# One block product in the first layer instead of two, turns from SBUF to SBUF, weight buffers of half a unit, and weight sums begun by an account of the transfers

## The chip, the cores and the metric

The kernel runs on one core of a Trainium2 chip. The metric is the device time of one execution in microseconds (us), the median of several runs. The engines named below are PE (TensorE, the matrix multiplications), DVE (VectorE), ACT (ScalarE), POOL (GpSimd) and SP (SyncE, which here only issues transfers). DMA engines carry the transfers; the queues of SP, ACT and POOL feed them.

## The reference

Two layers over 256 tokens of 2048 channels, float32. In each layer one wide projection (`w_in`, 2048 x 12304) makes the inputs of two groups of heads, a matrix memory (mLSTM) and a gated linear recurrence (RG-LRU); a second projection (`w_out`, 4096 x 2048) brings both back to 2048 channels.

```python
def hybrid_layer(x, ...):
    u = rms_norm(x, norm_g)
    p = u @ w_in
    qk, v, o, z_a, ig, fg, xb, z_b = jnp.split(p, SPLIT_AT, axis=-1)
    qk = silu(causal_dwconv(qk, qk_conv)); q, k = split(qk, 2)
    h = mlstm_chunkwise(q, k, v, ig + i_bias, log_sigmoid(fg + f_bias))
    h = h * sigmoid(o)                       # per head, then a norm over the head
    y_a = normed(h) * head_norm_g * silu(z_a)
    xc = causal_dwconv(xb, lru_conv_w) + lru_conv_b
    y_b = rg_lru(xc, w_a, b_a, w_x, b_x, lam) * silu(z_b)
    return x + concatenate([y_a, y_b]) @ w_out
# reference: two such layers, then a final rms_norm
```

## The kernel before

All products are float32 work done in three multiplications of rounded parts: each operand is split into a rounded part H (type fp32r) and the rest L, and `H*H + H*L + L*H` is summed in PSUM. The activations are split once per layer (`x_s`); the weights are split as they arrive: ACT casts `wH <- raw`, DVE subtracts `wL <- raw - wH`.

The weights come as 1 MB units, in the order in which they are used (`_sequence`). A unit is two halves of 512 KB. One plain half feeds 12 multiplications 128x512 (two token tiles, two slices of the contraction, three products), which PE works off in one go. Per layer there are four groups `g` of columns, each with the inputs `qk`, `v`, `o`, `z`, `xb`, `zb` of that group (four units each), the small gate products (`gate`, line 874), and the output projection of the group before (`out`). Loads are issued on SP into three buffers `raw` of one unit (`load_unit`, lines 339 and 341); splits run three halves ahead of PE (`AHEAD`), into four buffers `wH`, `wL`.

Block products: two columns of inputs of one layer (a pair in `PAIRS`) are multiplied together by seven block products instead of eight (a Strassen-Winograd scheme over two token tiles, two halves of the contraction and the pair). A pair has 7 x 4 = 28 block halves of 512 KB (`rawb`, loaded at line 349), each feeding 6 multiplications (lines 1229 to 1231, into the bank `ps_b`), where the plain form has 16 halves with 12 each. The block halves are placed among plain ones. The scheme needs sums of activation blocks (`block_sums`, on DVE, tiles `sums`, `sum_t`), an addition of each product into `res` (DVE), and sums of weight blocks in DRAM (`w_d`): `weight_sums` copies a block from the input into `w_d` (SP queue, line 1133) and adds further blocks by accumulating transfers (POOL queue, line 1142). It keeps a pace by PE's planned time (`PACE`: 6.5 us between transfers for the first layer, 10 for the second). Before, both pairs are done so in both layers: pair 0 is `v` and `o` of group 2, pair 1 is `o` and `z` of group 3.

A turn brings tokens on partitions to channels on partitions. ACT writes `tok`, DVE transposes blocks of 32x32 into `blk`, four transfers of 128 KB on SP (line 528) write a DRAM buffer `moved` with the blocks rearranged, and one transfer of 512 KB on POOL (line 529; the last turn on SP) reads it into `fr`. `fr` is then read by ACT (`ch`, `tok`, `zsg`) or DVE (`zb`). There are 35 turns. Their readers are placed by planned PE time (`LANDING` 10 us, `FAR` 15 us after the turn) and then by a scheduler that gives each engine its order.

Each engine and each queue works in order: what waits at the head holds back what is behind it. Transfers of one queue are counted on eight semaphores in rotation, and a transfer waits for the one eight before it on its queue.

Of the kernel before, what the change touches and what calls it, by code (L numbers as in the profile page):

```python
# [16 lines left out]
P = 128  # L17
# [15 lines left out]
PACE = 6.5, 10.0  # L33
# [64 lines left out]
def tile_trunk(ctx, tc, x, xt, par, gw, gb, ws, final_g, out):  # L98
# [22 lines left out]
    wraw = ctx.enter_context(tc.tile_pool(name="wraw", bufs=3))  # L121
# [7 lines left out]
    st = {"nload": 0, "lag": 0.0, "t": 0.0, "nprep": 0, "pair": 0, "aux": 0}  # L129
# [28 lines left out]
    def load_x_acc():  # L158
        new_x_acc()
        for c in range(4):  # L160
            nc.sync.dma_start(out=xa(c), in_=xd[c])

    def store_x(c):
        S.dma_start(out=xd[c], in_=xa(c))

# [157 lines left out]
    def load_unit(hf):  # L323
        n = st["nload"]
        st["nload"] += 1
        item, j = hf["at"]
        raw = hf["box"]["raw"] = wraw.tile([P, 2048], F32, tag="raw", name="raw")
        if n < 4:
            w = 512 if n == 0 else 1024
            u = blocks[item, j]  # L330
            for o in range(0, 2048, w):
                if o % 1024 == 0:
                    load_xt(n, o // 1024)
                nc.sync.dma_start(out=raw[:, o : o + w], in_=ws[u][:, o : o + w])
        elif hf["paired"]:
            o = 1024 * (j % 2)
            for s_ in range(2):
                u = blocks[item, 2 * s_ + j // 2]
                st["ld"] = nc.sync.dma_start(out=raw[:, 1024 * s_ : 1024 * s_ + 1024], in_=ws[u][:, o : o + 1024])
        else:  # L340
            st["ld"] = nc.sync.dma_start(out=raw, in_=ws[blocks[item, j]])
        if 3 <= n < 7:
            load_x(n - 3)

    def load_block(hf):
        if hf["made"]:
            require(hf["made"])
        raw = hf["raw"] = wblk.tile([P, 2, 512], F32, tag="rawb", name="rawb")
        st["ld"] = nc.sync.dma_start(out=raw.rearrange("p k n -> p (k n)"), in_=hf["from"])
        if "loaded" in hf:  # L350
            st[hf["loaded"]] = True

    def add_unit(mms, before=None, after=None, paired=False, own=None):
        box = {}
        halves.append([dict(box=box, i=i, mm=mms[i], split=None, paired=paired, own=own and own[i],
                            before=before if i == 0 else None, after=after if i == 1 else None) for i in range(2)])

    def prepare(hf):
        n = st["nprep"]
        if "from" not in hf:  # L360
# [5 lines left out]
            raw = hf["box"]["raw"]  # L366
        if "from" in hf:
            r = hf["raw"]
        elif hf["paired"]:
            r = raw.rearrange("p (s n) -> p s n", s=2)[:, :, 512 * hf["i"] : 512 * hf["i"] + 512]  # L370
        else:
            r = raw.rearrange("p (i n) -> p i n", i=4)[:, 2 * hf["i"] : 2 * hf["i"] + 2, :]
# [6 lines left out]
        for j, o in enumerate((slice(0, 1), slice(1, 2)) if opening else (slice(0, 2),)):  # L379
# [5 lines left out]
            if hf["own"] and "ends" in st:  # L385
                order(st["wH"], st["ends"][0])
                order(st["wL"], st["ends"][1])
        hf["split"] = (H.rearrange("p s n -> p (s n)"), L.rearrange("p s n -> p (s n)"))
# [129 lines left out]
    def swapped(tok, blk=None, back=G):  # L518
# [5 lines left out]
        st["lag"] += 1.2  # L524
        V.transpose(out=blk.rearrange("p m n -> p (m n)"), in_=tok.rearrange("p m c t j -> p (m c t j)"))
        moved = dram.tile([P, 4, 256], F32, tag="moved", name="moved", bufs=2)
        for a in range(4):
            nc.sync.dma_start(out=moved[:, a].rearrange("(m j) n -> j m n", m=4), in_=blk[32 * a : 32 * a + 32])
        i0 = back.dma_start(out=fr.rearrange("p a c t i -> p a (c t i)"), in_=moved)  # L529
# [479 lines left out]
    def out_chunk(l, g, c):  # L1009
# [9 lines left out]
        def postfn():  # L1019
            ps = acc()  # L1020
            if g < NG - 1:
# [3 lines left out]
                st["staged"] = st["n"]  # L1025
                return
# [38 lines left out]
    def block_sums(l):  # L1065
# [50 lines left out]
        yield from made(1, "S3", False, x(0, 0), x(1, 0), 4, (0, 3))  # L1116
        yield from made(1, "S1b", True, s(0), x(0, 0), 4, (1, 7))
        yield from made(0, "S4b", True, s(0), x(0, 1), 4, (1, 6))

    def block_unit(l, p, r, c, j):  # L1120
# [3 lines left out]
           for p in range(2)] for l in range(DEPTH)]  # L1124

    def weight_sums():

        def jobs(l, p):

            def copied(to, src, at, engine=nc.sync):  # L1130
                def f():
                    j, cs = at
                    i0 = engine.dma_start(out=wd[l][p][to][j][:, cs], in_=src(j)[:, cs])
                    order(i0, st["gq"] if engine is G else st["ld"])
                    if engine is G:
                        paced(i0, st["wH"])
                return f

            def added(to, src, at):
                def f():  # L1140
                    j, cs = at
                    i0 = G.dma_start(out=wd[l][p][to][j][:, cs], in_=src(j)[:, cs], accum_op=ALU.add)  # L1142
                    order(i0, st["gq"])
                    paced(i0, st["wH"])
                return f

            def b(r, c):
                return lambda j: block_unit(l, p, r, c, j)

            parts = [(j, slice(1024 * h, 1024 * h + 1024)) for j in range(2) for h in range(2)]  # L1150
            first, other, late = [], [], []
            for n, at in enumerate(parts):
                first += [(None, False, copied(0, b(0, 0), at), None), (None, True, added(0, b(0, 1), at), (5, n))]
                if p == 1:
                    first += [(None, True, copied(2, lambda j: wd[l][p][0][j], at, G), (5, n)),
                              (None, True, added(0, b(1, 1), at), (6, n))]
                else:
                    late.append((("loaded", l, p, 5, n), True, added(0, b(1, 1), at), (6, n)))
                other += [(None, False, copied(1, b(1, 1), at), None), (None, True, added(1, b(0, 1), at), (7, n))]
            late += [(("loaded", l, p, 6, n), True, added(0, b(1, 0), at), (4, n)) for n, at in enumerate(parts)]  # L1160
            return deque(first + other + late)

        queues = [jobs(l, p) for l in range(DEPTH) for p in range(2)]
        while st["n"] < SUMS_FROM:
            yield "wait"
        while any(queues):
            ready = [i for i, q in enumerate(queues) if q and (q[0][0] is None or q[0][0] in st)]
# [3 lines left out]
            i = ready[0]  # L1171
            _, adding, begin, made = queues[i].popleft()
            while adding and st["n"] - st.get("staged", -9) < 2 and not st.get("forced"):
                yield "wait"
            begin()
            if made:
                st[("made", i // 2, i % 2) + made] = True
            t0 = st["t"]
            while before(t0 + PACE[i // 2]):
                yield "wait"  # L1180
# [276 lines left out]
    for item, j in seq:  # L1457
        l, what = item[1], item[2:]
        if _blockwise(item):
            p = next(p for p in range(2) if what in PAIRS[p])  # L1460
# [5 lines left out]
    for l in reversed(range(DEPTH)):  # L1466
        for p in (1, 0):
# [19 lines left out]
    for n, hf in enumerate(order_):  # L1487
        st["n"] = n
        while nprep < len(order_) and nprep <= n + AHEAD:
            while st["nload"] < len(plain_) // 2 and st["nload"] <= (nplain + 5) // 2:  # L1490
                load_unit(plain_[2 * st["nload"]])
# [27 lines left out]
        st["t"] += took  # L1519
    drain()  # L1520
# [94 lines left out]
```

## Time and profile before

| | |
|---|---|
| median of 3 runs (1493.07 to 1495.65) | 1494.67 us |
| the profiled execution / its span | 1500.83 us / 1499.1 us |
| busy: PE / DVE / ACT / POOL | 98% / 80% / 65% / 9% of the span |
| granted TensorE clock, mean | 0.991 |
| moved by transfers | 425.39 MB, 284 GB/s over the span |

A busy PE here counts a multiplication from its start to its modelled end (390 ns), while the next one starts 0.227 us after it; so the share of 98% says little, and the number of multiplications in a stretch says more. Waits are put down to what ended last.

### The profile page before, as it was taken

How to read it: one execution, taken by the hardware profiler on the slowest of the kernel's cores; microseconds unless marked ns; L12 is line 12 of the kernel's file. 1: busy time of each engine (PE TensorE's matmuls, PEld its weight loads, DVE VectorE, ACT ScalarE, POOL GpSimd, SP SyncE). 2: the span in 40 equal slices, each digit the busy share in tenths (PEclk: the TensorE clock that was granted, in tenths of full speed). 3: DMA queues.
4: the chain of work that ended last, by engine and by line, in shares of the span. 5: the costliest groups of instructions: out<-in, count | busy, mean ns of one | idle time of the engine just before them, and what ended most of it. 6: DMA issues, size and time to landing. Idle time of an engine off the chain costs nothing. (4 is left out here: it accounts for less than half of the span.)

```text
span 1499.1 us, 19073 instructions
## 1 busy us (share of the span) xinstructions
PE 1470.4 (98%) x6734; PEld 1223.4 (82%) x6734; DVE 1194.8 (80%) x1678; ACT 981.2 (65%) x1256; POOL 142.0 (9%) x226
## 2 busy tenths in 40 slices
PE   9999999999989999999999999999999999999997
PEld 7888888888867888888887788888888888878876
DVE  5888898978677599877866888988787977888775
ACT  6666866567575667658564667665577757666665
POOL 0020101111101010000000200001000000000002
PEclk9999999999999999999999999999999999999999
DMA  9879999999999999899897787999978898777883
GB/s 353 325 257 277 302 306 301 323 318 287 333 282 281 295 312 313 289 304 305 295 331 230 228 289 250 309 283 296 290 264 299 259 268 265 271 262 239 248 303 109
DMA packets 117871, 425.39 MB, mean 284 GB/s; under 512 B 12928, under 2 KB 33424, under 8 KB 100368
## 3 DMA queue, kind: packets, MB, share of 16 engines
q1 hardware_dynamic: 95600, 348.39, 65.5%
q0 software_dynamic: 19712, 71.33, 21.9%
q10 hardware_dynamic: 2464, 4.47, 0.8%
q8 instruction: 52, 0.85, 0.2%
q14 instruction: 43, 0.35, 0.1%
HBM read 386.89 MB, written 91.77 MB: 319 GB/s over the span
## 5 line engine op out<-in xcount | busy, mean ns | idle before, releaser
L407 PE MATMUL acc<-wH,x_s 128*128 128x512 f32 x2496 | 786.1, 390 | 6.0 <-ACT wH L112 3.1
L112 DVE TENSOR_TENSOR wL<-raw,wH 128x1024 fp32r<-128x1024 f32 (+1 forms) x468 | 557.6, 1198 | 176.2 <-ACT wH L112 174.0
L112 ACT CAST wH<-raw 128x1024 fp32r<-128x1024 f32 (+1 forms) x468 | 481.0, 1035 | 289.0 <-PE acc L407 201.9
L407 PEld LDWEIGHTS acc<-wH,x_s 128*128 128x128 f32 x2496 | 469.7, 188 | 104.8 <-ACT wH L112 4.2
L407 PE MATMUL acc<-wL,x_s 128*128 128x512 f32 x1248 | 486.3, 391 | 3.5 <-DVE wL L112 3.5
L407 PEld LDWEIGHTS acc<-wL,x_s 128*128 128x128 f32 x1248 | 234.9, 188 | 53.4 <-DVE wL L112 5.3
L112 DVE TENSOR_TENSOR wL<-rawb,wH 128x1024 fp32r<-128x1024 f32 x112 | 136.4, 1218 | 38.7 <-ACT wH L112 38.6
L112 ACT CAST wH<-rawb 128x1024 fp32r<-128x1024 f32 x112 | 117.6, 1050 | 71.3 <-PE acc L407 47.2
L407 PE MATMUL acc<-wH,yaH 128*128 128x512 f32 x224 | 87.8, 392 | 0.0
L407 PE MATMUL acc<-wL,yaH 128*128 128x512 f32 x224 | 87.7, 391 | 0.0
L407 PE MATMUL acc<-wH,yaL 128*128 128x512 f32 x224 | 87.6, 391 | 0.0
L407 PE MATMUL acc<-wH,ybL 128*128 128x512 f32 x224 | 87.5, 390 | 0.0
L407 PE MATMUL acc<-wH,ybH 128*128 128x512 f32 x224 | 87.4, 390 | 0.0
L407 PE MATMUL acc<-wL,ybH 128*128 128x512 f32 x224 | 87.2, 389 | 0.0
L112 ACT ACT_TABLE_LOAD x63 | 80.8, 1283 | 9.4 <-DVE qc L112 3.5
L1142 POOL DMA_DIRECT2D w_d<-in_ws_dram x64 | 55.0, 859 | 298.9 <-ACT wH L112 183.4
L529 POOL DMA_DIRECT2D fr<-moved x34 | 19.3, 569 | 402.2 <-DMA moved<-blk 359.5
L112 DVE SCALAR_TENSOR_TENSOR qc<-ch,pars,qc 128x255 f32<-128x255 f32 (+2 forms) x96 | 42.3, 475 | 11.8 <-ACT qc L112 11.5
L1230 PE MATMUL ps_b<-wL,sums 128*128 128x512 f32 x128 | 50.0, 390 | 0.1
L1229 PE MATMUL ps_b<-wH,sums 128*128 128x512 f32 x128 | 50.1, 391 | 0.0
L1231 PE MATMUL ps_b<-wH,sums 128*128 128x512 f32 x128 | 49.9, 389 | 0.0
L407 PEld LDWEIGHTS acc<-wH,yaH 128*128 128x128 f32 x224 | 42.5, 190 | 8.9
(230 smaller groups left out, 1843.4 us busy)
## 6 DMA issues: line engine op xcount, KB each, us to landing
raw<-in_ws_dram SPq DMA_DIRECT2D x136, 1024.0 KB, 7.5
raw<-in_ws_dram SPq DMA_DIRECT2D x190, 512.0 KB, 6.8
w_d<-in_ws_dram POOLq DMA_DIRECT2D x64, 512.0 KB, 9.8
rawb<-w_d SPq DMA_DIRECT2D x64, 512.0 KB, 7.7
rawb<-in_ws_dram SPq DMA_DIRECT2D x48, 512.0 KB, 7.1
fr<-moved POOLq DMA_DIRECT2D x34, 512.0 KB, 7.4
moved<-blk SPq DMA_DIRECT2D x132, 128.0 KB, 4.4
w_d<-in_ws_dram SPq DMA_DIRECT2D x32, 512.0 KB, 8.6
```

The costliest lines, as they stand in the source:

```text
L112: ins = f(*a, **k)
L407: st["mm"] = PE.matmul(o, a_[:, kt, P * t : P * t + P], W[:, k], start=b, stop=z)
L529: i0 = back.dma_start(out=fr.rearrange("p a c t i -> p a (c t i)"), in_=moved)
L1142: i0 = G.dma_start(out=wd[l][p][to][j][:, cs], in_=src(j)[:, cs], accum_op=ALU.add)
L1229: PE.matmul(box["b"], aH, Hv[:, k], start=opening and k == 0, stop=False, skip_group_check=True)
L1230: PE.matmul(box["b"], aH, Lv[:, k], start=False, stop=False, skip_group_check=True)
L1231: PE.matmul(box["b"], aL, Hv[:, k], start=False, stop=kp == 3 and k == 1, skip_group_check=True)
```

## The change

Four things are changed. (1) `PRODUCTS = 1, 2`: the first layer has a block product for pair 0 alone; `o` and `z` of its group 3 go the plain way. (2) A turn no longer goes through DRAM: 16 transfers of 32 KB (32 partitions, 1 KB each) go from `blk` to `fr`, eight on SP and eight on POOL (all 16 on SP for the last one). (3) `raw` is six buffers of a half unit, each loaded by itself (`load_half`; the paired kinds `qk`, `xb`, `zb` by two transfers of 256 KB, the others by one of 512 KB). (4) `weight_sums` issues its copies too on POOL, in another order, and begins one when an account of transfer time, which each transfer raises and PE's planned time lowers, has room (`RATE`, `COPY`, `ADDING`, `TURN`), in place of `PACE`. The loads of `x_acc` are spread over eight halves.

```diff
-PACE = 6.5, 10.0
+RATE = 0.9, 0.75
+COPY, ADDING, TURN = 1.3, 2.6, 1.7
+PRODUCTS = 1, 2
...
-    return item[0] == "in" and any(item[2:] in pair for pair in PAIRS)
+    return item[0] == "in" and any(item[2:] in pair for pair in PAIRS[: PRODUCTS[item[1]]])
...
-    wraw = ctx.enter_context(tc.tile_pool(name="wraw", bufs=3))
+    wraw = ctx.enter_context(tc.tile_pool(name="wraw", bufs=6))
...
         for c in range(4):
-            nc.sync.dma_start(out=xa(c), in_=xd[c])
+            timed.append((st["n"] + 2 * c, lambda c=c: load_x_c(c)))
...
-    def load_unit(hf):
+    def load_half(hf):
         n = st["nload"]
         st["nload"] += 1
-        raw = hf["box"]["raw"] = wraw.tile([P, 2048], F32, tag="raw", name="raw")
+        (item, j), i = hf["at"], hf["i"]
+        raw = hf["raw"] = wraw.tile([P, 1024], F32, tag="raw", name="raw")
...
         elif hf["paired"]:
-            o = 1024 * (j % 2)
+            o = 1024 * (j % 2) + 512 * i
             for s_ in range(2):
                 u = blocks[item, 2 * s_ + j // 2]
-                st["ld"] = nc.sync.dma_start(out=raw[:, 1024 * s_ : 1024 * s_ + 1024], in_=ws[u][:, o : o + 1024])
+                st["ld"] = nc.sync.dma_start(out=raw[:, 512 * s_ : 512 * s_ + 512], in_=ws[u][:, o : o + 512])
         else:
-            st["ld"] = nc.sync.dma_start(out=raw, in_=ws[blocks[item, j]])
+            st["ld"] = nc.sync.dma_start(out=raw, in_=ws[blocks[item, j]][:, 1024 * i : 1024 * i + 1024])
+        st["dma"] += COPY
...
         V.transpose(out=blk.rearrange("p m n -> p (m n)"), in_=tok.rearrange("p m c t j -> p (m c t j)"))
-        moved = dram.tile([P, 4, 256], F32, tag="moved", name="moved", bufs=2)
-        for a in range(4):
-            nc.sync.dma_start(out=moved[:, a].rearrange("(m j) n -> j m n", m=4), in_=blk[32 * a : 32 * a + 32])
-        i0 = back.dma_start(out=fr.rearrange("p a c t i -> p a (c t i)"), in_=moved)
+        for m in range(4):
+            for a in range(4):
+                engine = nc.sync if m < 2 else back
+                i0 = engine.dma_start(out=fr[32 * m : 32 * m + 32, a].rearrange("p c t i -> p (c t i)"),
+                                      in_=blk[32 * a : 32 * a + 32, m])
...
+            def moved(to, src, at, **how):
+                def f():
+                    j, cs = at
+                    i0 = G.dma_start(out=wd[l][p][to][j][:, cs], in_=(wd[l][p][src][j] if src == 0 else block_unit(l, p, *src, j))[:, cs], **how)
+                    order(i0, st["gq"])
+                    paced(i0, st["wH"])
+                    st["dma"] += ADDING if how else COPY
+                return f
...
+            l, p, q = ready[0]
+            st["rate"] = RATE[l] if q[0][0] is None else 1.0
+            while (st["dma"] > (COPY if q[0][0] is None else ADDING) or st["n"] - st.get("staged", -9) < 2) and not st.get("forced"):
                 yield "wait"
...
-            while st["nload"] < len(plain_) // 2 and st["nload"] <= (nplain + 5) // 2:
-                load_unit(plain_[2 * st["nload"]])
+            while st["nload"] < len(plain_) and st["nload"] <= nplain + 5:
+                load_half(plain_[st["nload"]])
...
         st["t"] += took
+        st["dma"] = max(0.0, st["dma"] - took * st["rate"])
```

Three places show what it moves. The first is ACT at the turn of `qk` of group 2 in the first layer: `tok_...` begins the turn, `ch_...<-fr_...` reads it, the casts `wH` between them feed PE. Before:

```order
L112 ACTIVATE tok_3522<-acc_3326,rstd_465 128x4x4x32 x2
L112 CAST wH_3536<-rawb_3405 128x1024
L112 CAST wH_3548<-raw_3392 128x1024
L112 CAST wH_3568<-raw_3392 128x1024
L112 CAST wH_3584<-rawb_3482 128x1024
L112 ACT_TABLE_LOAD
L112 ACTIVATE E_3594<-E_3594 128x768
L112 CAST wH_3604<-raw_3447 128x1024
L112 CAST wH_3633<-raw_3447 128x1024
L112 CAST wH_3653<-raw_3503 128x1024
L112 CAST wH_3669<-rawb_3546 128x1024
L112 COPY ch_3621<-fr_3526 128x1024
```

And now, the same turn:

```order
L114 ACTIVATE tok_3743<-acc_3540,rstd_477 128x4x4x32 x2
L114 CAST wH_3770<-rawb_3621 128x1024
L114 CAST wH_3782<-raw_3607 128x1024
L114 CAST wH_3801<-raw_3639 128x1024
L114 CAST wH_3819<-rawb_3703 128x1024
L114 ACT_TABLE_LOAD
L114 ACTIVATE E_3829<-E_3829 128x768
L114 CAST wH_3839<-raw_3665 128x1024
L114 COPY ch_3855<-fr_3747 128x1024
```

The reader of the turn stood behind eight casts (five of plain halves, three of block halves) and now stands behind five (three and two).

The second place is POOL around the same turn (`E` is a mask for the attention scores, `nb` a broadcast load). Before:

```order
L529 DMA fr_3314<-moved_3316 128x1024
L1142 DMA w_d0101_126<-in_ws_dram 128x1024 x2
L1133 DMA w_d0121_130<-w_d0101_126 128x1024
L665 AFFINE_SELECT E_3594<-E_3594 128x128 x4
L529 DMA fr_3526<-moved_3528 128x1024
L1142 DMA w_d0101_126<-in_ws_dram 128x1024
L1142 DMA w_d0110_127<-in_ws_dram 128x1024
L529 DMA fr_3765<-moved_3767 128x1024
```

And now:

```order
L532 DMA fr_3515<-blk_3514 32x256 x8
L654 DMA nb_3765<-nG_d0_119 128x512
L696 MEMSET vH_3972 128x4x2
L1140 DMA w_d1001_126<-in_ws_dram 128x1024
L1140 DMA w_d1000_125<-in_ws_dram 128x1024
L532 DMA fr_3747<-blk_3746 32x256 x8
L669 AFFINE_SELECT E_3829<-E_3829 128x128 x4
L1140 DMA w_d1001_126<-in_ws_dram 128x1024 x2
L532 DMA fr_4002<-blk_4001 32x256 x8
```

POOL's part of the turn has moved ahead of the mask, it is eight transfers instead of one, and it no longer waits for a transfer of SP.

The third place is SP there. Before:

```order
L339 DMA raw_3447<-in_ws_dram 128x1024 x2
L349 DMA rawb_3482<-w_d0001_122 128x1024
L339 DMA raw_3503<-in_ws_dram 128x1024 x2
L528 DMA moved_3528<-blk_3525 32x4x256 x4
L349 DMA rawb_3546<-w_d0001_122 128x1024
L341 DMA raw_3566<-in_ws_dram 128x2048
L1133 DMA w_d0110_127<-in_ws_dram 128x1024
L341 DMA raw_3629<-in_ws_dram 128x2048
```

And now:

```order
L344 DMA raw_3724<-in_ws_dram 128x512 x2
L344 DMA raw_3767<-in_ws_dram 128x512 x2
L532 DMA fr_3747<-blk_3746 32x256 x8
L355 DMA rawb_3780<-w_d0001_122 128x1024
L346 DMA raw_3799<-in_ws_dram 128x1024
L346 DMA raw_3817<-in_ws_dram 128x1024
L355 DMA rawb_8315<-in_ws_dram 128x1024
L346 DMA raw_3863<-in_ws_dram 128x1024
```

Eight transfers of the turn stand ahead of the loads where four stood, a load is a half unit, and the copy of a weight block (`w_d`) is gone from SP. Over the whole program PE has 192 multiplications of the plain form more and 168 of the block form less; ACT has 12 casts `wH` less, DVE 12 subtractions `wL` less; SP issues 423 transfers more, POOL 242 more.

More of the change, by code (lines that the diff above doesn't have):

```diff
@@ L160, in load_x_acc, with load_x_c @@
         for c in range(4):
-            nc.sync.dma_start(out=xa(c), in_=xd[c])
+            timed.append((st["n"] + 2 * c, lambda c=c: load_x_c(c)))
+    def load_x_c(c):
+        order(nc.sync.dma_start(out=xa(c), in_=xd[c]), st["ld"])
+        st["dma"] += COPY
     def store_x(c):
         S.dma_start(out=xd[c], in_=xa(c))
+        st["dma"] += COPY
     new_x_acc()
@@ L365, in prepare @@
                 st["nprep"] += 1
[L366 to L372, printed above, removed]
+        r = hf["raw"]
+        if "from" not in hf:
+            r = r.rearrange("p (s n) -> p s n", s=2)
         if hf["own"]:
@@ L1025, in postfn @@
                 st["staged"] = st["n"]
+                st["dma"] += ADDING
                 return
@@ L1160, in jobs, with copied, added @@
-            late += [(("loaded", l, p, 6, n), True, added(0, b(1, 0), at), (4, n)) for n, at in enumerate(parts)]
-            return deque(first + other + late)
-        queues = [jobs(l, p) for l in range(DEPTH) for p in range(2)]
+            def copied(to, src, n):
+                return None, moved(to, src, parts[n]), None
+            def added(to, src, n, no, loaded=None):
+                return loaded and ("loaded", l, p, loaded, n), moved(to, src, parts[n], accum_op=ALU.add), (no, n)
@@ new lines, in pair @@
+            def pair(to, a, b, no):
+                c, d = [copied(to, a, n) for n in range(4)], [added(to, b, n, no) for n in range(4)]
+                return [c[0], c[1], d[0], c[2], d[1], c[3], d[2], d[3]]
+            parts = [(j, slice(1024 * h, 1024 * h + 1024)) for j in range(2) for h in range(2)]
+            early = pair(0, (0, 0), (0, 1), 5)
+            second = [added(0, (1, 1), n, 6, 5 if p == 0 else None) for n in range(4)]
+            late = [added(0, (1, 0), n, 4, 6) for n in range(4)]
@@ new lines, in jobs @@
+            other = pair(1, (1, 1), (0, 1), 7)
+            if p == 1:
+                kept = [(None, moved(2, 0, at), (5, n)) for n, at in enumerate(parts)]
+                between = [job for n in range(3) for job in (kept[n + 1], second[n])]
+                return deque(late), deque(early + kept[:1] + between + second[3:] + other)
+            return deque(second + late), deque(early + other)
+        queues = [(l, p, q) for l in range(DEPTH) for p in range(PRODUCTS[l]) for q in jobs(l, p)]
@@ L1459, in tile_trunk @@
         if _blockwise(item):
-            p = next(p for p in range(2) if what in PAIRS[p])
+            p = next(p for p in range(PRODUCTS[l]) if what in PAIRS[p])
             ends[l, p] = len(order_)
@@ L1466, in tile_trunk @@
     for l in reversed(range(DEPTH)):
-        for p in (1, 0):
+        for p in reversed(range(PRODUCTS[l])):
             a, b = ends[l, p - 1], ends[l, p]
```

68 lines of the change are left out of this document (22 added, 46 removed).

## The prediction

> **What bounds the kernel now.** I read the page first, then PE's waits, stretches of time by window, and the timelines of ACT, SP and POOL around PE's waits.
>
> ```profile
> span 1499.1 us, 19073 instructions
> PE 1470.4 (98%) x6734; PEld 1223.4 (82%) x6734; DVE 1194.8 (80%) x1678; ACT 981.2 (65%) x1256; POOL 142.0 (9%) x226
> L112 DVE TENSOR_TENSOR wL<-rawb,wH 128x1024 fp32r<-128x1024 f32 x112 | 136.4, 1218 | 38.7 <-ACT wH L112 38.6
> L112 ACT CAST wH<-rawb 128x1024 fp32r<-128x1024 f32 x112 | 117.6, 1050 | 71.3 <-PE acc L407 47.2
> ...
> 810.29 16.36 PE acc L407 x72
> 896.79 4.20 PE ps_gt L874 x36
> ```
>
> The last two rows are from the chain that ended last: 72 multiplications in 16.36 us, so one 128x512 costs PE 0.227 us, and a narrow one of the gates 4.20/36 = 0.117 us. ACT's casts wait mostly for PE: PE is the bound wherever it is fed. By window:
>
> ```profile
> core 0: us, PE busy (x), PEclk, DMA share, GB/s
> 100.00:400.00 300.00, 300.00 (x1394) 1.00 0.97 305
> 860.00:1320.00 460.00, 460.00 (x2129) 1.00 0.88 280
> 375.00:400.00 25.00, 25.00 (x112) 1.00 1.02 334
> 412.00:422.00 10.00, 5.12 (x15) 0.83 0.71 155
> 449.00:459.00 10.00, 5.90 (x17) 0.66 0.95 251
> 679.00:688.00 9.00, 5.78 (x29) 0.81 1.01 307
> 795.00:804.00 9.00, 6.05 (x20) 0.81 0.50 177
> 850.00:853.00 3.00, 2.06 (x8) 1.00 0.05 20
> 1329.00:1336.00 7.00, 6.17 (x27) 1.00 0.60 210
> 1442.00:1449.00 7.00, 5.14 (x15) 0.76 0.42 142
> ```
>
> For 760 us PE has no gap, even with the DMA engines 0.97 busy. A dense stretch of 25 us shows 112 multiplications, 1.9 more than 25/0.227, which are those across its edges. So each other window lost its length less (x - 1.9) x 0.227: A (412) 7.0, B (449) 6.6, D (795) 4.9, E (850) 1.6, F (1329) 1.3, G (1442) 4.0 us; C (679), where 18 are narrow, 9 - 18 x 0.117 - 9.1 x 0.227 = 4.8. Together 30.2 us of PE time, and nothing else between the first microseconds and the tail is to be had. The clock fell after most of these waits, and this is inside the numbers. What ended the waits ahead of them:
>
> ```profile
> 412.48 1.04 ACT L112 COPY ch<-fr 128x1024 f32<-128x1024 f32 x1 [6.68 <-DMA fr<-moved]
> 442.70 1.05 ACT L112 COPY ch<-fr 128x1024 f32<-128x1024 f32 x1 [5.09 <-DMA fr<-moved]
> 676.83 1.05 ACT L112 CAST wH<-raw 128x1024 fp32r<-128x1024 f32 x1 [4.23 <-DMA raw<-in_ws_dram]
> 792.20 1.05 ACT L112 CAST wH<-raw 128x1024 fp32r<-128x1024 f32 x1 [5.94 <-DMA raw<-in_ws_dram]
> 1437.76 1.71 ACT L112 ACTIVATE tok<-fr,pars 128x256 f32<-128x256 f32 x4 [4.49 <-DMA fr<-moved]
> 776.89 1.71 ACT L112 ACTIVATE tok<-fr,pars 128x256 f32<-128x256 f32 x4 [3.00 <-DMA fr<-moved]
> ```
>
> A, B and G are late turns: ACT works in order, so the casts that PE needs next are queued behind the reader of `fr`, and DVE's subtractions behind the casts. C and D are late weights. The wait of 3.00 us at 776.89 cost PE nothing until 795: the splits run three halves ahead, so ACT may be some 3 to 4 us late for free.
>
> **The change, part by part.** *The plain form in the first layer.* 192 multiplications more, 168 less: 24 x 0.227 = **+5.45 us**, all on PE, which sets the end; nothing hides it. The 12 splits less (1.05 us each on ACT, 1.22 on DVE), and the sums on DVE, are off the path: 0 saved by themselves, but they make room for the casts after a late turn. One half of weights then lasts 2.72 us on PE instead of 1.36, so from about 460 to 650 us the demand for loads falls to half.
>
> *The turns.*
>
> ```profile
> 390.89 3.92 SPq L528 DMA_DIRECT2D moved<-blk  x4
> 426.56 2.05 SPq L528 DMA_DIRECT2D moved<-blk  x4
> 432.90 0.58 POOL L529 DMA_DIRECT2D fr<-moved  x1 [15.97 <-DMA moved<-blk]
> L528 SPq DMA_DIRECT2D moved<-blk x132: 302/436/2405, 59.9 to 1451.3; - x132
> DMA to landing us min/median/max: 2.0/4.5/10.9
> L529 POOL DMA_DIRECT2D fr<-moved x34: 527/564/721, 64.7 to 1429.3; - x34
> DMA to landing us min/median/max: 3.6/7.4/9.8
> ```
>
> Turn A took from 390.89 to 412.48, 21.6 us; turn B from 426.56 to 442.70, 16.1. The new turn has one leg. On SP the eighth issue is at 7 x 0.436 = 3.1 us, and a piece like these lands 4.5 us later: 7.6 us. On POOL the eighth issue is at 7 x 0.564 = 3.9 us; a landing is bounded by 3.6 us (the shortest there) and 7.4 (the median of a transfer sixteen times as large): 7.5 to 11.3 us. I take 9, nearer the lower end, since a piece is small. But the order also puts the reader nearer: five casts instead of eight behind `tok`, by PE's pace 3 x 2.72 + 2 x 1.36 = 10.9 us instead of 17.7, of which
>
> ```profile
> 423.58 1.24 ACT L112 ACTIVATE tok<-acc,rstd 128x512 f32<-128x512 f32 x2
> 425.30 1.23 DVE L112 STREAM_TRANSPOSE blk<-tok 128x1024 f32<-128x1024 f32 x1
> ```
>
> 2.95 us pass before SP can begin. So 8 us are left for a turn of 7.5 to 11.3: ACT waits 0 to 3.3 us there, within what is free. A and B go, up to a rest at those of the 35 turns that come late: I keep 3.5 of the 13.6 us, **-10.1 us**. For the tightly placed turns the margin stays thin.
>
> Behind POOL's eight issues (4.5 us instead of 0.56) stand the mask, the broadcast and the additions to `x_d`; at 9% busy POOL has the time, and who waits for the mask waits later than for the turn: 0, at most those 4 us once. Behind SP's eight stand the loads.
>
> *Half-unit buffers.*
>
> ```profile
> raw<-in_ws_dram SPq DMA_DIRECT2D x136, 1024.0 KB, 7.5
> raw<-in_ws_dram SPq DMA_DIRECT2D x190, 512.0 KB, 6.8
> SPq L341 <- DVE wL L112: 341.4, 94, 13.5
> ```
>
> SP waits for DVE to free a buffer, not for the DMA engines. A unit's buffer was free when its second half was split, and its next content was needed five halves later, 13.6 us, less 7.5 to land: 6.1 us of slack. A half buffer is needed six halves later, 16.3 less 6.8: 9.5 us. The 3.4 us more would leave 0.8 of the wait of 4.23 at C and 2.5 of the 5.94 at D. As SP's turn now stands ahead of the loads for 3.5 us and not 1.7, I take 5.5 of the 9.7 us: **-5.5**. The bounds are 0 and -9.7. The 423 issues more cost SP 0.44 us each by the row of the turns, 186 us, under the 341 us that it waits anyway; where that cover is gone, right behind a turn, is the second rival.
>
> *Sums by an account.* 32 copies leave SP, 76 transfers are on POOL instead of 72, 28 fewer in all. In the new order at least 140 multiplications stand between the last addition to a piece and its load, so none is waited for: 0. For E, F and G (6.9 us), G a late turn again, I take half: **-3.5**.
>
> **The sum.** 5.45 - 10.1 - 5.5 - 3.5 = -13.65. The profiled execution is 1500.83 us, its span 1499.1; the median of the runs is 1494.67, 6.2 less, and I take the difference over to it unchanged: **1481 us**. Were every wait to go, it would be 1494.67 + 5.45 - 30.2 = 1469.9, the lower end; with A and B gone alone (-13.6), 1486.5.
>
> The price of a new wait is its length and the slow clock behind it: at A the waits of PE itself were 4.9 of the 7.0 us.
>
> ```profile
> PE acc L407 <- DVE wL L112: 3.5, 3, 1.8
> PE acc L407 <- ACT wH L112: 3.1, 1, 3.1
> ```
>
> The Trainium skill ("TensorE: Matmul & The Clock Gate", "What's actually happening") says that the clock halves only after an idle window of about 3.4 us. Here it also fell at G (0.76), after waits of about 1 us in two pieces, so the row decides, and small waits are charged at more than their length; by the page's rule, G would have cost 2 us and not 4.0.
>
> **The rivals.** *The pieces come one behind another* (chance 0.14). If the eight pieces of a queue do not overlap, a turn is 8 x 4.5 = 36 us at worst by the row of 128 KB. Against it: at B four were issued within 2.05 us, and POOL was released 4.3 us after the last. From about 15 us per turn on, A and B stay; then 5.45 - 5.5 + 0 leaves 1494.6, no change. The Trainium skill ("DMA: Bandwidth & Descriptors", "Rules for kernel authors") speaks for this rival: transfers under 64 KB are mostly overhead and should be joined, with a fixed cost of about 2 us each. As an estimate from that page, eight in a row would be 8 x 2.08 = 16.6 us, the same side as turn B before. No run so far shows pieces of 32 KB.
>
> *SP's turn holds back the loads* (0.16; slower). A queue's transfer waits for the one eight before it, so a turn fills SP's rotation, and the next load waits for the first piece: 3.5 + 4.5 = 8.0 us, under the slack of 9.5. If a piece takes its longest, 10.9, it is 14.4: loads come 4.9 us late, and PE pays up to 7, as at A. It decides where this eats the 13.65 us of the sum and the 3 us that can be told: 16.65/7, so from three turns of the 35 on; three give 1481 + 21 = 1502, four 1509.
>
> *Loads stay late* (0.2). If at C and D it is the DMA engines that are late (C shows them 1.01 busy) and not the buffer, finer buffers change nothing. C and D stay, A and B go: 1486.5, perhaps 1490 with a little lost at the nearer readers.
>
> The forecast (1470 to 1485) has 0.5.
>
> **How the numbers follow.** A measurement of this kernel tells 0.2%, 3 us, from no change. Faster: the forecast and the third rival, and a little of the first, 0.72. Same: most of the first, 0.12. Slower: the second, 0.16. The range from 1470 to 1498 leaves out the worse half of the second rival and a little below the lower end.
>
> **What would show it.** Right: PE has 24 multiplications more; windows near 390 to 460 hold 110 per 25 us; ACT's waits for `fr` stay under 4 us each, where three of those shown were above; a turn lands within 8 to 12 us of `blk`; casts' waits for `raw` fall below the 41.8 us of before. Wrong: new waits of PE behind `ch<-fr` in the tight turns, or casts that wait for `raw` just after a turn on SP.
>
> ```profile
> ACT wH L112 <- DMA raw<-in_ws_dram: 41.8, 20, 5.9
> ```

## The result and the profile after

The changed kernel took 1482.68 us (median of 4 runs, 1480.39 to 1485.29) beside 1495.16 us of the kernel before: a ratio of 0.9914, with a 95% interval from 0.9888 to 0.994. It is faster by 12.5 us, and 1481 had been predicted. The sum came out right; the runs below show that its terms did not.

The head of the page of the changed kernel, and its windows (the columns are PE, weight loads, DVE, ACT and POOL busy, the granted clock, the busy share of the DMA engines and GB/s):

```profile
span 1478.7 us, 20749 instructions
PE 1466.1 (99%) x6758; PEld 1222.1 (83%) x6758; DVE 1168.8 (79%) x1621; ACT 970.2 (66%) x1241; POOL 251.3 (17%) x468
...
DMA packets 155533, 386.23 MB, mean 261 GB/s; under 512 B 23568, under 2 KB 35360, under 8 KB 155424
...
380.00:460.00 80.00, 78.09 (x352) 64.70 (x351) 63.63 (x92) 54.14 (x67) 14.69 (x27) 1.00 0.90 285
460.00:660.00 200.00, 200.00 (x918) 166.97 (x917) 131.27 (x161) 119.45 (x143) 31.04 (x57) 1.00 0.85 252
660.00:700.00 40.00, 40.00 (x234) 35.29 (x233) 33.93 (x52) 32.95 (x47) 5.35 (x10) 1.00 0.86 254
700.00:860.00 160.00, 159.49 (x708) 130.76 (x707) 126.25 (x177) 96.72 (x134) 40.65 (x78) 1.00 0.84 259
1320.00:1460.00 140.00, 139.92 (x652) 116.87 (x651) 114.79 (x158) 94.94 (x118) 13.40 (x23) 1.00 0.74 233
```

The same windows of the profiled execution of before:

```profile
380.00:460.00 80.00, 71.02 (x296) 57.77 (x295) 58.30 (x78) 51.62 (x65) 8.07 (x14) 0.94 0.96 296
460.00:660.00 200.00, 200.00 (x927) 167.27 (x926) 165.47 (x251) 130.75 (x156) 18.37 (x27) 1.00 0.94 301
660.00:700.00 40.00, 36.78 (x197) 31.90 (x196) 24.09 (x25) 26.76 (x41) 3.22 (x4) 0.96 0.99 314
```

PE has the 24 multiplications more (x6758 against x6734), and where A to G stood it is fed but for 1.9 us near B: 78.09 of 80 us instead of 71.02 (352 multiplications, 110 per 25 us, as forecast), 40.00 of 40 instead of 36.78, the clock at 1.00 in all these windows. The DMA engines are 0.90, 0.85 and 0.86 busy where they were 0.96, 0.94 and 0.99. The longest wait that is left to PE, what ACT still waits for, and the pieces of a turn:

```profile
PE ps_S L752 <- DVE Pt L114: 2.1, 2, 1.9
```

```profile
ACT wH L114 <- DMA raw<-in_ws_dram: 24.5, 26, 4.7
...
ACT ch L114 <- DMA fr<-blk: 6.9, 3, 3.1
```

The row of `ch` in the kernel before:

```profile
ACT ch L112 <- DMA fr<-moved: 24.9, 9, 6.7
```

And the pieces:

```profile
L532 SPq DMA_DIRECT2D fr<-blk x272: 507/588/1564, 63.1 to 1440.3; - x136
L532 POOL DMA_DIRECT2D fr<-blk x256: 496/498/677, 63.4 to 1410.0; - x128
...
DMA to landing us min/median/max: 1.7/3.4/9.3
```

Casts' waits for `raw` fell from 41.8 us to 24.5, those of `ch` for `fr` from 24.9 to 6.9. Over all of ACT's tiles the waits for `fr` fell less, from 41.5 to 25.9 us; the longest is 3.1 us, where it was 6.7. The eighth issue of SP is at 7 x 0.588 = 4.1 us and a piece lands 3.4 us later: 7.5 us. Taken turn by turn (end of the transpose to the last landing that the trace records), the median of the 35 turns is 7.7 us, where it was 13.4.

Nearly all of PE's waits are gone, then: 4.4 us in sum beside 20.0. Which of the four parts did it? The experiments take them out of the changed kernel one by one, and put them into the kernel before. The kernel before took between 1487 and 1504 us in the 63 runs beside them, so ratios with their intervals are compared, not single times.

### The profile page after: what moved, and what is told of

Read it like the earlier page. It is cut to its first block, busy times and chain, and to the rows that moved or that the text cites. A ratio compares the mean times of both kernels' runs of the same rounds, so it can differ in the third digit from the quotient of the medians.

```text
span 1478.7 us, 20749 instructions
## 1 busy us (share of the span) xinstructions
PE 1466.1 (99%) x6758; PEld 1222.1 (83%) x6758; DVE 1168.8 (79%) x1621; ACT 970.2 (66%) x1241; POOL 251.3 (17%) x468
## 2 busy tenths in 40 slices
DMA packets 155533, 386.23 MB, mean 261 GB/s; under 512 B 23568, under 2 KB 35360, under 8 KB 155424
## 4 chain that ended last, share of the span: by engine, by line
PE 81%; DMA 8%; DVE 5%; ACT 2%; SPq 2%; issue 2%; POOL 0%; DVEq 0%; ACTq 0%
PE acc L409 68%; DMA raw<-in_ws_dram 5%; PE ps_b L1232 3%; PE ps_b L1233 3%; PE ps_b L1234 3%; PE ps_gt L878 2%; DVE wL L114 2%; SPq L532 1%; DMA xp<-in_xt_dram 1%; DMA x_d<-x_acc 1%; DMA fr<-blk 1%; ACT wH L114 1%; DMA x_acc<-in_x_dram 1%; DVE scs L114 1%; PE ps_n L677 0%
## 5 line engine op out<-in xcount | busy, mean ns | idle before, releaser
L409 PE MATMUL acc<-wH,x_s 128*128 128x512 f32 x2624 | 821.7, 389 | 0.2 <-ACT wH L114 0.2
L114 DVE TENSOR_TENSOR wL<-raw,wH 128x1024 fp32r<-128x1024 f32 (+1 forms) x484 | 578.8, 1200 | 201.3 <-ACT wH L114 199.2
L409 PEld LDWEIGHTS acc<-wH,x_s 128*128 128x128 f32 x2624 | 492.4, 188 | 102.3 <-ACT wH L114 0.8
L409 PE MATMUL acc<-wL,x_s 128*128 128x512 f32 x1312 | 509.5, 389 | 0.0
L532 POOL DMA_DIRECT2D fr<-blk x256 | 126.8, 506 | 357.8 <-DVE blk L114 188.6
L114 DVE TENSOR_TENSOR wL<-rawb,wH 128x1024 fp32r<-128x1024 f32 x84 | 102.4, 1219 | 26.8 <-ACT wH L114 26.8
L114 ACT CAST wH<-rawb 128x1024 fp32r<-128x1024 f32 x84 | 88.3, 1051 | 52.6 <-PE acc L409 35.2
L409 PEld LDWEIGHTS acc<-wH,ybL 128*128 128x128 f32 x224 | 42.1, 188 | 9.8 <-DVE ybL L988 1.0
L409 PEld LDWEIGHTS acc<-wH,yaL 128*128 128x128 f32 x224 | 42.0, 188 | 8.8
L409 PEld LDWEIGHTS acc<-wH,ybH 128*128 128x128 f32 x224 | 42.0, 188 | 8.7 <-ACT ybH L987 0.3
```

The costliest lines, as they stand in the source:

```text
L114: ins = f(*a, **k)
L409: st["mm"] = PE.matmul(o, a_[:, kt, P * t : P * t + P], W[:, k], start=b, stop=z)
L532: i0 = engine.dma_start(out=fr[32 * m : 32 * m + 32, a].rearrange("p c t i -> p (c t i)"), in_=blk[32 * a : 32 * a + 32, m])
```

## Experiments: one part taken out

**The turn through DRAM again.**

```diff
-                i0 = engine.dma_start(out=fr[32 * m : 32 * m + 32, a]..., in_=blk[32 * a : 32 * a + 32, m])
+            nc.sync.dma_start(out=moved[:, a]..., in_=blk[32 * a : 32 * a + 32])
+        i0 = back.dma_start(out=fr..., in_=moved)
```

> The changed kernel with one part undone: a turn goes through DRAM again (four transfers of 128 KB on SP, one of 512 KB on POOL). Everything else, the nearer places of the readers too, stays as changed. Theory (the short turn cured A and B, 10.1 of the forecast): the turns need 16 to 22 us again while their readers stand where a turn of 11 us is wanted, so A and B come back, in the median about 8 to 10 us: 1490 to 1493 us, and ACT's waits for fr rise from the 26 us of the changed kernel to over 40. Rival (A and B went since the first layer asks for half the loads from 460 us on, or since the sums collide less): the way of a turn hardly matters, 1481 to 1486 us, waits for fr not longer than 4 us each.

Measured: 1498.18 us, ratio to before 1.0026 (1.0008 to 1.0045). Its waits of PE and ACT:

```profile
PE ps_S L751 <- DVE Pt L114: 6.6, 3, 3.5
PE acc L409 <- DVE wL L114: 2.9, 2, 1.8
```

```profile
ACT wH L114 <- DMA raw<-in_ws_dram: 22.9, 21, 2.5
ACT ch L114 <- DMA fr<-moved: 22.4, 8, 4.6
```

The theory's wait came back: `ch` waits 22.4 us for `fr` instead of 6.9, and PE waits 1.8 us at A and 3.5 at B. Over all of ACT's tiles the waits for `fr` are 32.3 us beside 25.9, not the 40 that were expected. The 18 MB that go through DRAM again (404.50 MB in all) do not make the loads late: casts wait for `raw` as little as in the changed kernel, and a load of 512 KB lands in 6.2 us in the median beside 6.7. So the turn is needed where the readers now stand. The cost, 15 us, is larger than the 8 to 10 expected. At G nothing came back (PE is busy for 140.00 of 140 us from 1320 to 1460), so there the turn is not what is needed.

**Whole-unit buffers again.**

```diff
-    wraw = ctx.enter_context(tc.tile_pool(name="wraw", bufs=6))
+    wraw = ctx.enter_context(tc.tile_pool(name="wraw", bufs=3))
... load_unit as before, two entries in the account
```

> The changed kernel with one part undone: three weight buffers of a whole unit in place of six of half a unit. Theory (the buffer came free too late; 5.5 us of the forecast): casts wait for raw again around 680 and 795 us, 1486 to 1490 us, and ACT's waits for raw rise from 24.5 us to about 40. Rival (the DMA engines were late, and what lightened them was the missing block product and the turns that no longer go through DRAM): 1481 to 1485 us with the waits for raw where they are.

Measured: 1498.88 us, ratio 1.0023 (0.9999 to 1.0047).

```profile
PE ps_gt L885 <- ACT gate L890: 5.6, 4, 2.4
PE acc L416 <- DVE wL L114: 3.4, 5, 0.9
```

```profile
ACT wH L114 <- DMA raw<-in_ws_dram: 63.2, 29, 5.6
```

Waits for `raw` rose from 24.5 to 63.2 us, more than in the kernel before (41.8): the new turn needs finer buffers. The theory's places are wrong: PE does not wait from 670 to 700 us nor near 795. The losses are many small waits over the span, the largest at the gates.

**The second block product back in the first layer.**

```diff
-PRODUCTS = 1, 2
+PRODUCTS = 2, 2
```

> The changed kernel with one part undone: both block products in both layers again, so 24 x 0.227 = 5.45 us less on PE. Theory (turns and buffers cured the waits, the missing product only cost): 1482.7 - 5.45 = 1477 us, between 1475 and 1479.5, faster than both kernels. Rival (the plain form paid for itself by halving the demand for loads between 460 and 650 us and taking 28 transfers of sums away): waits for loads or for the sums' additions come back there, 1483 to 1492 us.

Measured: 1549.89 us, ratio 1.0372 (1.0335 to 1.0409). Neither number expected was near. PE and SP show why:

```profile
PE ps_b L1232 <- ACT wH L114: 33.2, 5, 9.7
```

```profile
SPq L355 <- DMA w_d<-in_ws_dram: 93.8, 12, 15.8
```

SP stands up to 15.8 us at a block load whose sum is not yet made, and with it all the loads behind. The account is set for the smaller number of sums. The same kernel with one more pair of numbers changed:

```diff
-RATE = 0.9, 0.75
+RATE = 1.0, 0.9
```

> The changed kernel with both block products in both layers, which took 1549.9 us, and with one pair of numbers changed: the account falls by 1.0 and 0.9 of PE's planned time instead of 0.9 and 0.75. With the old numbers 36 of the sums were begun only when their load already stood at the head of SP, and SP waited 93.8 us for them; with the new ones none is begun so late. Theory (most of the 67 us was the account): 1549.9 - 40 or more, 1490 to 1512 us, and no wait of SP for w_d. Rival (both products cannot be fed, whenever the sums begin): above 1525 us, with waits of casts for rawb over 5 us. If turns and buffers alone had cured the waits it would be 1477 us, faster than both kernels; after the run with both products at the fixed pace (1516 us) this has little chance.

Measured: 1515.36 us, ratio 1.0136 (1.0108 to 1.0163). Both expectations missed the time, which lies between them. SP no longer waits for `w_d`, and 34.5 us are gone; some 20 us above before remain, though PE has 5.45 us less to do than in the changed kernel. The rival's sign is there: casts wait for `rawb` up to 6.9 us. The loss of PE lies in many small waits, the largest sum of them:

```profile
PE acc L409 <- DVE wL L114: 7.6, 10, 1.6
```

**The sums at a fixed pace again.**

```diff
+PACE = 6.5, 10.0
... weight_sums as before: copies on SP, one transfer each PACE of planned time
```

> The changed kernel with one part undone: the weight sums begin at a fixed pace (6.5 and 10 us of planned time) again, with copies on SP and the order of before. Theory (the sums were costed at 0): 1480 to 1486 us. Rival (the account keeps accumulating transfers away from turns and loads, and that is where the 25 us of waits went that the profiled execution lost): SP's copies and unplaced additions make loads or turns late, 1487 us or more, and single waits for raw or fr over 5 us.

Measured: 1491.86 us, ratio 0.9986 (0.997 to 1.0001).

```profile
ACT wH L115 <- DMA raw<-in_ws_dram: 32.6, 28, 4.0
```

The way in which the sums are begun, costed at 0, is worth some 10 us, on the rival's side, though no single wait of ACT for `raw` or `fr` reached 5 us. Three things changed together here, the account, the queue of the copies and the order of the sums; which of them it is stays open.

## Experiments: one part put in

**The new turn alone.** The kernel before with the last lines of `swapped` as changed:

```diff
-        moved = dram.tile([P, 4, 256], F32, tag="moved", name="moved", bufs=2)
-        ... four transfers to moved on SP, one to fr on POOL
+        for m in range(4):
+            for a in range(4):
+                engine = nc.sync if m < 2 else back
+                i0 = engine.dma_start(out=fr[32 * m : 32 * m + 32, a]..., in_=blk[32 * a : 32 * a + 32, m])
```

> The kernel before with one part of the change alone: turns go from SBUF to SBUF by 16 transfers of 32 KB. Taken out of the changed kernel, this part cost 1498.2 - 1482.7 = 15.5 us. Theory (the turns are worth their late readers at A, B and G by themselves): alone it gives about 10 us, ratio 0.991 to 0.996, and ACT waits for fr under 4 us each. Rival (the parts only work together: with whole-unit buffers SP's eight issues ahead of the loads make the loads late): ratio 0.998 to 1.005, and ACT's waits for raw rise above the 41.8 us of before while those for fr fall.

Measured: 1518.78 us, ratio 1.0149 (1.0124 to 1.0174): slower, beyond the rival's range, though turns became shorter (a median of 8.4 us). Its waits, and SP, POOL and ACT at the place of A:

```profile
ACT wH L112 <- DMA raw<-in_ws_dram: 91.9, 34, 8.5
```

```profile
SPq L529 <- DMA raw<-in_ws_dram: 22.6, 16, 3.5
```

```profile
402.23 9.50 SPq L529 DMA_DIRECT2D fr<-blk  x8
```

```profile
407.86 0.54 POOL L1134 DMA_DIRECT2D w_d<-w_d  x1 [8.58 <-DMA raw<-in_ws_dram]
408.63 3.46 POOL L529 DMA_DIRECT2D fr<-blk  x7 [0.22 <-issue]
413.26 0.50 POOL L529 DMA_DIRECT2D fr<-blk  x1 [1.17 <-DMA fr<-blk]
```

```profile
420.98 1.04 ACT L112 COPY ch<-fr 128x1024 f32<-128x1024 f32 x1 [8.84 <-DMA fr<-blk]
```

SP's pieces wait for loads of up to 1 MB (22.6 us in 16 waits), at A its eight issues take 9.50 us, and all the while no load is issued: casts wait 91.9 us for `raw`. But the changed kernel shows the same on SP, and its casts wait 24.5 us:

```profile
SPq L532 <- DMA raw<-in_ws_dram: 24.9, 29, 3.3
```

```profile
392.95 7.65 SPq L532 DMA_DIRECT2D fr<-blk  x8
```

So the pieces on SP do not make `raw` late by themselves; the loads behind them are whole units here and halves there, and the changed kernel has fewer of them and of the sums. On POOL the pieces stand behind a transfer of the sums that itself waits 8.58 us, so A comes even later than before (8.84 us against 6.68).

**The same with all 16 pieces on POOL.**

```diff
-                engine = nc.sync if m < 2 else back
+                engine = back
```

> The kernel before with the new turn alone, but all 16 pieces on POOL and none on SP. With eight on SP that kernel took 1518.8 us, ACT's waits for raw were 91.9 us, and SP's pieces waited for transfers of loads (a piece waits for the transfer eight before it on its queue): at turn A SP's eight issues took 9.5 us. Theory (the pieces on SP hold back the loads, and wait for them): waits for raw return to about 42 us and the time to 1490 to 1502 us, though 16 issues of 0.47 us make each turn about 11 us long. Rival (the small pieces load the DMA engines, or POOL's queue with its additions is the late one): 1510 us or more, and waits for fr longer than before.

Measured: 1576.15 us, ratio 1.0545 (1.0517 to 1.0573).

```profile
ACT ch L112 <- DMA fr<-blk: 58.7, 11, 9.3
ACT wH L112 <- DMA raw<-in_ws_dram: 46.1, 21, 5.9
```

```profile
POOL fr L529 <- DMA fr<-blk: 56.9, 48, 3.5
```

The part of the theory on the loads is borne out: without pieces on SP, the waits for `raw` are 46.1 us, not 91.9 (in a kernel that is 57 us longer, which gives the loads more time too). The time went the rival's way: the ninth piece on a queue waits for the first to land (56.9 us in 48 waits), a turn takes 15.1 us in the median, and `ch` waits 58.7 us.

**Half-unit buffers alone.** `load_half` and six buffers in the kernel before:

```diff
-    wraw = ctx.enter_context(tc.tile_pool(name="wraw", bufs=3))
+    wraw = ctx.enter_context(tc.tile_pool(name="wraw", bufs=6))
-                load_unit(plain_[2 * st["nload"]])
+                load_half(plain_[st["nload"]])
```

> The kernel before with one part of the change alone: six buffers of half a unit. Taken out of the changed kernel, this part cost 16.2 us. Theory (a buffer came free too late): alone it takes away the late weights at C and D, ratio 0.994 to 0.998, and ACT's waits for raw fall from 41.8 to 25 us or less. Rival (that cost was due to the account and the near readers, which are set for finer loads): ratio 0.999 to 1.002 with waits for raw near 40 us.

Measured: 1514.42 us, ratio 1.0104 (1.0079 to 1.0128), outside both. ACT's waits, and ACT at the place of C:

```profile
ACT wH L112 <- DMA raw<-in_ws_dram: 33.5, 24, 5.6
ACT ch L112 <- DMA fr<-moved: 27.5, 7, 7.4
ACT tok L112 <- DMA fr<-moved: 13.8, 6, 6.1
ACT stage L112 <- DMA x_d<-stage: 10.3, 1, 10.3
```

```profile
685.31 1.05 ACT L112 CAST wH<-raw 128x1024 fp32r<-128x1024 f32 x1 [3.70 <-DMA raw<-in_ws_dram]
```

Casts wait a little less for `raw` in sum (33.5 us), but C stays: 3.70 us where it was 4.23, and PE waits 1.5 us at the gates there. And turns and the store of `stage` became later. The windows show the DMA engines fuller than before (0.96 to 1.01 from 380 to 700 us); that this is the reason is argued, not shown.

**One block product less alone.** The kernel before, with the sums at their pace:

```diff
+PRODUCTS = 1, 2
-    return item[0] == "in" and any(item[2:] in pair for pair in PAIRS)
+    return item[0] == "in" and any(item[2:] in pair for pair in PAIRS[: PRODUCTS[item[1]]])
```

> The kernel before with one part of the change alone: the first layer has one block product instead of two. With the second product put back into the changed kernel it took 67 us more, where 5.45 less were expected. Theory (that loss came from the account, which begins the transfers of the sums too late when there are 28 more of them; by itself the plain form only costs its 24 multiplications): ratio 1.002 to 1.005. Rival (the plain form pays for itself, since the demand for loads falls by half over 190 us and the sums of the second layer can begin earlier): ratio 0.985 to 0.998, and casts no longer wait for raw between 400 and 690 us.

Measured: 1494.23 us, ratio 0.9989 (0.9971 to 1.0008): it costs nothing. ACT at the place of C, and the window around it:

```profile
672.87 1.05 ACT L113 CAST wH<-raw 128x1024 fp32r<-128x1024 f32 x1 [2.75 <-PE acc L408]
```

```profile
660.00:700.00 40.00, 40.00 (x233) 35.16 (x232) 32.44 (x56) 29.61 (x43) 2.23 (x3) 1.00 0.76 223
```

C is gone here, with whole-unit buffers, and the DMA engines are 0.76 busy there instead of 0.99. This is no chance of one execution: PE waits 1.0 to 3.7 us at the gates of C in each of the seven traces of kernels that have both products and the fixed pace (two of the kernel before, five of versions of it), and not at all in the five traces with one product. So the missing product, not the buffers, is what brought the weights of C in time here, and it paid for its 5.45 us. It is not the only thing that can: with both products and the account that wait is gone too, in kernels that lose more elsewhere. The theory is refuted; the time is between the two, though the interval reaches the rival's range. The rival's sign failed: between 400 and 690 us casts wait 17.4 us for `raw`, more than the 8.0 of before, but PE does not wait for them.

**Turn and buffers together.** The diffs of the new turn alone and of the half-unit buffers alone, both in the kernel before.

> The kernel before with two parts of the change: turns from SBUF to SBUF and half-unit buffers; both block products in both layers, and the sums at their fixed pace. It is the fair counterpart of the run with both products and the account. Theory (turns and buffers cured the waits, the missing product only cost, the 67 us were the account's): 1482.7 - 5.45 us or a little more, ratio 0.987 to 0.991, faster than the changed kernel. Rival (without the plain form the first layer asks for more than the queues bring): ratio 0.995 or above, with casts waiting for raw and rawb between 400 and 690 us.

Measured: 1516.31 us, ratio 1.0131 (1.0102 to 1.0161): the rival. Waits for `raw` fell from 91.9 to 47.1 us beside the new turn alone, but the time hardly moved (1.0149 there): the sum of ACT's waits is not the price. Casts wait 25.0 us for `rawb<-w_d`.

```profile
ACT wH L112 <- DMA raw<-in_ws_dram: 47.1, 29, 5.9
ACT wH L112 <- DMA rawb<-w_d: 25.0, 9, 7.0
```

**The same without the sums of that product.**

```diff
+        which = [(l, p) for l in range(DEPTH) for p in range(2) if (l, p) != (0, 1)]
-        queues = [jobs(l, p) for l in range(DEPTH) for p in range(2)]
+        queues = [jobs(l, p) for l, p in which]
... its loads take single blocks of the input
```

> The kernel before with turns from SBUF to SBUF and half-unit buffers (1516.3 us), and with one thing left out of the computation: no weight sums are made for the second block product of the first layer, its block halves load single blocks from the input instead. PE's multiplications, their order of kinds and the number of loads stay; 28 transfers of 512 KB go. Dropping that product altogether (with the account not yet in) gave 1491.9 us although it adds 5.45 us on PE, so it was worth 30 us of waits. Theory A (the sums' transfers did it, in the DMA engines and in POOL's and SP's queues): 1485 to 1497 us. Theory B (the demand of 28 halves at 1.36 us each on loads, ACT and DVE did it): 1507 us or more, with PE's waits between 400 and 620 us as they were.

Measured: 1498.12 us, ratio 1.0021 (1.0002 to 1.0039), 1 us above the range of theory A. Of the 0.0145 between both products (1.0131) and one (0.9986, the sums at the pace), leaving out the sums is 0.0110, 16 us. By which way is not separated: 28 transfers go from the DMA engines and from POOL's and SP's queues (the loads of 512 KB land in 7.4 us in the median instead of 8.3), and block loads need not wait for their sums (casts wait 12.9 us for `rawb<-w_d` instead of 25.0). The other 5 us, and the 5.45 us of PE that the plain form adds, are left for the demand of the block halves for loads, casts and subtractions, and for the spread loads of `x_acc`. At C the sums are not the cause, since the wait stays without them, as long as in the first profile of before (3.2 us):

```profile
PE ps_gt L868 <- ACT gate L873: 3.2, 1, 3.2
```

**The kernel before once more**, for a second profile.

> The kernel before, unchanged, for a second profile. The profiled execution that the prediction was worked out from took 1500.83 us, the runs since from 1487 to 1504. Theory (the same waits come in every execution, since the order of each queue is fixed): waits of PE at A, B, C and D again, each within 1.5 us of the first profile, about 36 us of PE time lost over the span. Rival (the waits depend on how long transfers take in an execution): two or more of the seven are absent or less than half as long, and the loss of PE goes with the time of the execution.

Measured: 1490.52 us, span 1487.9. Three waits of PE in the first profile of before, and then those of the second and one of its windows:

```profile
PE ps_S L748 <- DVE Pt L112: 4.1, 1, 4.1
PE ps_gt L874 <- ACT gate L879: 3.2, 1, 3.2
...
PE acc L407 <- ACT so L112: 3.0, 1, 3.0
```

```profile
PE acc L407 <- DVE wL L112: 4.2, 5, 1.8
PE ps_S L748 <- DVE Pt L112: 3.7, 1, 3.7
PE acc L1350 <- ACT wH L112: 1.7, 1, 1.7
PE ps_gt L874 <- ACT gate L879: 1.5, 1, 1.5
```

```profile
380.00:460.00 80.00, 74.05 (x313) 60.24 (x313) 60.15 (x79) 52.67 (x66) 8.72 (x14) 0.96 0.98 313
```

B (3.7 us beside 4.1) is there again. At C the wait is 1.5 us instead of 3.2; at A the 3.1 us for `wH` are gone and only a wait for `wL` (up to 1.8 us) is left; at D the 3.0 us for `so` are gone. That is the rival's sign: how much the same order of instructions loses differs between executions. ACT's longest waits for `raw` and `fr` were 5.9 and 6.7 us in the first profile and are 3.3 and 5.5 here, while the median landing of the loads of 512 KB is the same (6.8 us); so it would be single transfers, which is argued, not shown.

## Why the prediction was right, and where its steps were not

**The steps, from the kernel before to the changed one** (ratio to before after the step, and the difference in us of 1495.2; each ratio is known to 2 to 4.5 us):

| step | ratio | difference | predicted |
|---|---|---|---|
| turn and half-unit buffers | 1.0131 | +19.6 | -15.6 |
| one block product less | 0.9986 | -21.7 | +5.45 |
| sums by the account | 0.9914 | -10.8 | 0 |
| all | 0.9914 | -12.9 | -13.65 with E, F, G |

The step from 1.0131 to 0.9986 also holds the spread loads of `x_acc`, which weren't tried apart. Nor is the account apart from the queue and the order of the sums. In another order the shares would be others: alone, the missing product gives nothing that can be told, and with all the rest in place 33 us (1.0136 to 0.9914, the account set anew). The parts share one resource, the slack of the loads and turns, and are no terms that add.

**The plain form, +5.45.** The multiplications are there (x6758). What failed is the step that booked them alone. The prediction had seen that the demand for loads falls to half from 460 us on, and gave it no price. Right: PE pays 5.45 us. Missing: the 28 transfers of sums that go with the product (16 us, with half-unit buffers and the new turn), and the demand of 28 block halves.

**The turns, -10.1.** Their size was right: 9 us estimated within 7.5 to 11.3, 7.7 measured (13.4 before). SP's issue was mis-sized (0.588 us each, not 0.436), the landing too (3.4, not 4.5), against each other. With the changed kernel's other parts the turn is worth what was said and more (15 us when it is undone). The step that failed is the cover: "behind SP's eight stand the loads" was left to a rival of 0.16. In the kernel before that rival is simply what happens (91.9 us of waits for `raw`, 1518.8 us, where 1502 to 1509 had been worked out). The changed kernel escapes it with smaller loads and fewer of them and of the sums together: with whole units it takes 1498.88 us, with both products 1515.36. That fewer bytes under way (386.23 MB instead of 425.39) are the reason is argued; SP's pieces wait for loads as long as in the slow version (24.9 us beside 22.6).

**Half-unit buffers, -5.5.** The reading "a buffer came free too late" of C was wrong: with the buffers alone C keeps 3.70 of 4.23 us, with one product less and the old buffers it goes. The third rival, that the DMA engines are late there (1.01 busy), fits what was seen, but not the consequence that it drew, that C would stay: another part of the same change relieved them (0.76 busy with one product less alone). That it is their share that counts, and not the halved demand at ACT and DVE, no run shows. The finer buffers are needed all the same, for the new turn: without them `raw` costs 63.2 us of waits.

**Sums, 0.** Mis-sized by some 10 us. It was asked only whether a load waits for its sum. What was not asked is what stands behind a sum's transfer on POOL: now half a turn does (8.58 us at A in the kernel with the new turn alone). Whether that is where the 10 us went is not shown.

**E, F and G, -3.5.** In the changed kernel PE is busy for all but 0.6 us of the two windows that hold them (700 to 860 and 1320 to 1460 us), so they went. But G was read as a late turn, and with the turn through DRAM again it stays away.

**The pieces one behind another** (0.14). On two queues they overlap. The Trainium skill ("DMA: Bandwidth & Descriptors", "Rules for kernel authors") would join transfers under 64 KB; the estimate from it, 16.6 us a turn, is not what the rows show (7.7 us). With 16 on one queue it comes close (15.1 us), but there the rows name another cause, the wait for the piece eight before.

**From the profile to the median.** The 6.2 us were taken over unchanged. After the change the profiled execution is 2.3 us below its median, so the traces differ by 20.4 us and the medians by 12.5. The second profile of before shows what the first held: beside the changed kernel it lost 1499.1 - (1478.7 - 5.45) = 25.9 us more in waits, the second 14.7. Had the sum taken all 25.9 us, the same transfer would have given 1494.67 + 5.45 - 25.9 = 1474 us. Recovering too little and starting from too much cancelled each other: that 1481 came so near is in part luck, and the number is better than its working.

## What to carry to other kernels

Before a wait for a transfer is put down to a buffer, a queue or an engine, look at the busy share of the DMA engines in that window. Where it is near 1, as at C (0.99), taking transfers away can be worth more than finer buffers, even when it adds work on the engine that bounds the kernel. A high share alone is no sign of a loss: from 100 to 380 us it was 0.97 in the kernel before, and PE had no gap. Transfers on a shared in-order queue are to be costed with both neighbours, what they wait for and what waits for them; the same short turn cost 22 us in one surrounding and gained 15 us in another. And one profile is not the median: a wait seen in one execution can be half as long, or absent, in the next. Where several edits use one slack, take the total of the waits as the bound of the gain, and do not book it edit by edit.

## What the runs showed of the hardware

The waits of one kernel before differ by 11 us between two executions whose instructions stand in the same order, most at A, C and D. The pieces of 32 KB take SP longer to issue (0.588 us) than those of 128 KB did (0.436), and POOL a little less than one of 512 KB did (0.498 against 0.564). One piece lands anywhere from 1.7 to 9.3 us after its issue in the changed kernel; what lies ahead of it in the DMA engines was not separated.

The longest wait of PE that is left in the changed kernel, 1.9 us up to 444.88 us, did not lower the clock:

```profile
436.00:446.00 10.00, 8.09 (x39) 6.55 (x38) 6.72 (x12) 4.69 (x7) 0.86 (x1) 1.00 1.04 315
```

It is 1.00 there. The Trainium skill ("TensorE: Matmul & The Clock Gate", "What's actually happening") has the clock fall only after some 3.4 us, which agrees here and did not at G before, where it was 0.76 after two waits of about 1 us. The second profile of before shows that the length of the wait does not decide alone: at G it has two longer waits (1.7 and 1.2 us) and the clock is 1.00 from 1430 to 1440, at A it has one of 1.8 us and the clock is 0.83 from 412 to 422. What decides stays open.

None of the versions tried is faster than the changed kernel.
